# Splitting the first v tiles earlier, keeping worked-ahead tiles for behind the gates, writing the last gates in two pieces, beginning the rows by index later

## The chip, the core and the metric

The kernel runs on one core of a Trainium2 chip. The metric is the time of one execution in device microseconds. Before the change it is the median of three executions; beside these stands one profiled execution, whose trace is read below. TensorE multiplies, VectorE, ScalarE (ACT) and GpSimd (POOL) work on tiles in SBUF, SyncE (SP) issues most of the transfers, POOL those by index.

## What is computed

The reference runs two layers of a hybrid trunk: a normalised and modulated input projection, three token mixers, a gated merge, and then the part that the change touches, an expert layer with product keys. For every token, 8 heads choose 16 of 16,384 experts each, and the experts' rows of u and v are used:

```python
act = gelu(einsum('td,thkd->thk', xb, u[ib]))
out = einsum('thk,thkd->td', gb * act, v[ib])
```

with ib the chosen indices and gb a softmax over the 16 scores. The first layer has 512 tokens (256 latent, 256 of context), the second 256. The output is the latent stream after a last norm.

## The kernel before

**Dense instead of gathered.** The kernel doesn't fetch rows for most tokens. It works through all 128 tiles of 128 experts: for tile i1 it forms gelu(u x h) for all tokens, multiplies with a gate (zero for experts that a token did not choose), and adds the product with v to sums in PSUM. Products are made of three matmuls on float32r halves: a tile is split into a high part (a cast on ACT) and a low part (a subtraction on VectorE or POOL). In the first layer the first 128 tokens go another way, by index: 128 rows of u and 128 rows of v are fetched for all of them by POOL, each worked on by VectorE. The list todo holds these steps (4 groups of 32, with a step for the gelu of each group), 260 in all; function due tells how many of them are to be done by tile i1, from tile GA on over GB tiles, with a weight of 2 for tiles 0 to 15 and 26 to 111 and of 1 for the others. Dense are thus TD = 384 tokens in the first layer and 256 in the second.

**The gates.** Function spread builds the gates, 128 tokens per call, 32 (TB) per buffer stg, four per step. A step makes a one-hot tile o2 (on VectorE, one time in eight on ACT), four tiles o1 on VectorE, four matmuls into one bank of PSUM, and a copy by ACT into stg. When stg is full it is written to Gd in DRAM, 2 MB: 12 writes in the first layer, 8 in the second. Behind the last one the loop over groups of GS = 4 tiles loads Gt, the gates of four tiles, out of all blocks of Gd.

**Tiles worked ahead.** While gates are made, TensorE has work in between: early_tiles forms gelu(u x h) for the first NP = 26 tiles (NA of their results lie in pool uv, NX in pool ux), each by 8 plain float32 matmuls, which the trace records as 16, reading h2f, the unsplit copy of h. Function fill(n) advances them by n matmuls. 11 tiles (NR) go ahead of the routing, the rest is spread evenly over the steps of spread. fill and spread put their matmuls in one order by hand (at_, issue_after). Other instructions are ordered by the framework's scheduler, which keeps no strict program order among engines' queues: a load may be issued earlier than the lines say.

**Buffers.** Weight tiles are loaded into wr and split into whi and wlo, in turn from the pools in raws and parts. In the expert part the first layer has two buffers of each, the second three. dp, the pool of the last loop (gS and gacc in the first layer, then Gt with two buffers, ah, al, three each of vr, vh, vl, and four of gr for the rows by index), is opened after the pools of h2f and of the gates are closed, and so takes their room; a new tile waits for the readers of an old one that lay in its place.

**The loop.** For each tile: the activation (worked ahead, or by wload and mm3), the product with the gate on VectorE, the cast ah on ACT, the rest al on VectorE, the load and split of v in vparts, and, one tile behind, vstage: 6 matmuls per 128 tokens.

Of the kernel before, what the change touches and what calls it, by code (L numbers as in the profile page):

```python
# [22 lines left out]
TB = 32  # L23
OH = "DDDDDDDA"

GA, GB = 2, 118


PRE = ((16, 10, 11), (26, 0, 11))
HALF = ("100100", "000100")  # L30
HALF = [[int(c) for c in h] for h in HALF]
HB = 2
# [11 lines left out]
def hybrid_trunk(ctx: ExitStack, tc: tile.TileContext, xin, cin, ccol, vecs, rows, ada_w, ada_s, w_in, rpb, w_up, w_out,  # L44
                 wq, keys, u, un, v, consts, out, dbg=None):
    nc = tc.nc
    PE, ACT, DVE, POOL, SP = nc.tensor, nc.scalar, nc.vector, nc.gpsimd, nc.sync
# [11 lines left out]
    def nm(s):  # L59
        cnt[0] += 1  # L60
        return f"{s}_{cnt[0]}"
# [155 lines left out]
    def wload(src, k=8, e=None, behind=None):  # L217

        wn[0] += 1
        raw = raws[wn[0] % len(raws)].tile([128, 8, 128], F32, name=nm("wr"), tag="wr")  # L220
        last["load"] = SP.dma_start(raw[:, :k], src).ins
        p = parts[wn[0] % len(parts)]
        hi = p.tile([128, 8, 128], F32R, name=nm("whi"), tag="whi")
        lo = p.tile([128, 8, 128], F32R, name=nm("wlo"), tag="wlo")
        e = e or (DVE if wn[1] and wn[0] % wn[1] == 0 else POOL)
        with tc.issue_after(behind) if behind is not None else nullcontext():
            ACT.copy(hi[:, :k], raw[:, :k])  # L227
        if half[0]:
            DVE.tensor_tensor(lo[:, :k // 2], raw[:, :k // 2], hi[:, :k // 2], op=OP.subtract)  # L229
            e.tensor_tensor(lo[:, k // 2:k], raw[:, k // 2:k], hi[:, k // 2:k], op=OP.subtract)  # L230
        else:
            e.tensor_tensor(lo[:, :k], raw[:, :k], hi[:, :k], op=OP.subtract)  # L232
        return hi, lo
# [41 lines left out]
    for l in range(NL):  # L275
        ctx_out = l < NL - 1
        T = 512 if ctx_out else 256
        NT = T // 128
# [16 lines left out]
        with ExitStack() as st:  # L295
            npool = pool(st, "np")
            if l == 0:
# [14 lines left out]
                for s in range(2):  # L312
                    for hf in range(2):
                        p = bcast_cols(sc_[:, :, s], 4 * hf, 4, "pm")
# [83 lines left out]
        with ExitStack() as st:  # L398
# [71 lines left out]
            for j in (4, 5, 6, 7, 8, 9, 10, 11, 0, 1, 2, 3):  # L470
# [9 lines left out]
                else:  # L480
                    DVE.scalar_tensor_tensor(a, th, 1.0, a, op0=OP.add, op1=OP.mult)
                    p = PS()
# [507 lines left out]
        G0 = 128 if ctx_out else 0  # L990
        TD = T - G0
        NBK = TD // TB
        NA, NX, NR = PRE[l]
        NP = NA + NX
        uv = pool(hst, "uv", 2)
        if G0:
# [171 lines left out]
        def early_tiles():  # L1168

            for i1 in range(NP):  # L1170
                wn[0] += 1
                raw = raws[wn[0] % len(raws)].tile([128, 8, 128], F32, name=nm("wr"), tag="wr")
                SP.dma_start(raw, u[l, i1])
                p = PM()
                for k in range(8):
                    e = PE.matmul(p[:, 0:TD], raw[:, k], h2f[:, k, G0:T], start=k == 0, stop=k == 7).ins  # L1176
                    if k == 7:
                        a = act_tile(i1)
                        last["gelu"] = ACT.activation(a, p[:, 0:TD], AF.Gelu).ins  # L1179
                        pre_acts.append(a)  # L1180
                    yield e

        fills = early_tiles()
        at_ = [None, 0, 0]

        def fill(n):

            for _ in range(n):
                with tc.issue_after(at_[0]) if at_[0] is not None else nullcontext():
                    e = next(fills, None)  # L1190
                if e is None:
                    return
                at_[0] = e
                at_[1] += 1

        def spread(t, iT):

            for b in range(128 // TB):
                stg = sp2.tile([128, 128, TB], F32, name=nm("stg"), tag="stg", bufs=2)
                for c in range(TB // 4):  # L1200
                    p = PS()
                    n = TB * b + 4 * c
                    o2 = sp2.tile([128, 4, 128], F32, name=nm("o2"), tag="o2", bufs=4)
                    how = OH[c % 8]
                    if how == "A":
                        for i in range(4):
                            ACT.activation(o2[:, i], iota, AF.Abs, scale=-1.0, bias=iT[:, 2, n + i:n + i + 1])
                        ACT.activation(o2, o2, AF.Relu, scale=-1.0, bias=1.0)
                    else:
                        DVE.tensor_tensor(o2, iota.unsqueeze(1).to_broadcast([128, 4, 128]),  # L1210
                                          iT[:, 2, n:n + 4].unsqueeze(2).to_broadcast([128, 4, 128]),
                                          op=OP.is_equal)
                    for i in range(4):
                        o1 = sp2.tile([128, 128], F32, name=nm("o1"), tag="o1", bufs=8)
                        DVE.tensor_scalar(o1, iota, iT[:, 1, n + i:n + i + 1], iT[:, 0, n + i:n + i + 1],
                                          op0=OP.is_equal, op1=OP.mult)
                        with tc.issue_after(at_[0]):
                            at_[0] = PE.matmul(p[:, 128 * i:128 * i + 128], o2[:, i], o1, start=True, stop=True).ins  # L1218
                    ACT.copy(stg[:, :, 4 * c:4 * c + 4].rearrange("p i t -> p t i"),
                             p.rearrange("p (t i) -> p t i", t=4))  # L1220

                    at_[2] += 1
                    fill(8 * NR + -(-8 * (NP - NR) * at_[2] // (TD // 4)) - at_[1])
                SP.dma_start(Gd[(128 // TB) * t + b - G0 // TB], stg)

        rt_ = {}
        fill(8 * NR)
# [6 lines left out]
        with ExitStack() as st:  # L1234
            sp2 = pool(st, "sp2", side="right")
            for t in range(G0 // 128, NT):
                spread(t, rt_[t])
        it_st.close()
        hf_st.close()
# [2 lines left out]

        pst_ps = ExitStack()
        ps_pools(pst_ps, ps=8 - NPM)
        GS = 4
        half[0] = HALF[l][5]
        dp = pool(hst, "dp", 2)
        todo = []
# [52 lines left out]
                                  stop=i1 == 127 and n == 2)  # L1301

        def vparts(i1):
            vr = dp.tile([128, 1024], F32, name=nm("vr"), tag="vr", bufs=3)
            SP.dma_start(vr, v[l, i1])
            vh = dp.tile([128, 1024], F32R, name=nm("vh"), tag="vh", bufs=3)
            vl = dp.tile([128, 1024], F32R, name=nm("vl"), tag="vl", bufs=3)
            split(vr, vh, vl, e_lo=DVE)
            return vh, vl

        ntodo = len(todo)
        for g in range(128 // GS):
            Gt = dp.tile([128, NBK, GS, TB], F32, name=nm("Gt"), tag="Gt")
            SP.dma_start(Gt.rearrange("p b e t -> p b (e t)"),
                         Gd[:, :, GS * g:GS * g + GS, :].rearrange("b p e t -> p b (e t)"))
            for e in range(GS):
                i1 = GS * g + e
                if i1 < NP:
                    a = pre_acts[i1]
                else:  # L1320
                    uh, ul = wload(u[l, i1], e=DVE if ctx_out else None)
                    p = PM()
                    mm3(p[:, 0:TD], uh, ul, h2h, h2l, (G0, T))
                    a = act_tile(i1)
                    last["gelu"] = ACT.activation(a, p[:, 0:TD], AF.Gelu).ins  # L1325
                DVE.tensor_tensor(a.rearrange("p (b t) -> p b t", t=TB), a.rearrange("p (b t) -> p b t", t=TB),  # L1326
                                  Gt[:, :, e, :], op=OP.mult)
                ah = dp.tile([128, TD], F32R, name=nm("ah"), tag="ah", bufs=5)
                al = dp.tile([128, TD], F32R, name=nm("al"), tag="al", bufs=5)
                ACT.copy(ah, a)  # L1330
                ev = DVE.tensor_tensor(al, a, ah, op=OP.subtract)  # L1331
                acts.append((i1, ah, al) + vparts(i1))
                if i1:
                    vstage(*acts.pop(0))

                n = len(todo) - ntodo + due(i1)
                for f, j in todo[:n]:
                    with tc.issue_after(ev.ins):
                        f(j)
                del todo[:n]  # L1340
                if NX and i1 == NP:

                    ux_st.close()
                    xst = ExitStack()
                    xT = pool(xst, "xp", side="right").tile([128, 8, 512], F32, name=f"xr{l}")
                    SP.dma_start(xT, xs2)
            if G0 and g == 30:
                for hf in range(2):
                    p = PM()
                    for k in range(4):  # L1350
                        PE.transpose(p[:, 128 * k:128 * k + 128], gacc[:, 512 * hf + 128 * k:512 * hf + 128 * k + 128],
                                     ident)
                    for k in range(4):
                        d = 4 * hf + k
                        DVE.scalar_tensor_tensor(xT[:, d, 0:128], p[:, 128 * k:128 * k + 128], mod[:, 40 + d, 0:1],
                                                 xT[:, d, 0:128], op0=OP.mult, op1=OP.add)
# [142 lines left out]
```

## Time and profile before

| what | us |
|---|---|
| median of 3 executions | 3756.54 (3756.0 to 3765.81) |
| the profiled execution's own time | 3751.19 |
| its span, first to last instruction | 3749.4 |
| TensorE busy | 3549.1 (95% of the span) |
| VectorE busy | 2710.7 (72%) |
| ACT busy | 1553.2 (41%) |
| POOL busy | 988.5 (26%) |

All times inside the trace count from the start of the span. A busy TensorE is not a TensorE at its peak, since ends of matmuls are modelled. The gates of the first layer lie between some 1073 and 1238 us, those of the second between 2973 and 3084; the loop over the tiles follows each.

### The profile page before, as it was taken

The page shows a single profiled execution, that of the slowest core. Times are in us where ns is not written, and L with a number is a line of the kernel's source. Part 1 is how long each engine was busy: PE and PEld are TensorE (multiplying, and loading weights), DVE is VectorE, ACT ScalarE, POOL GpSimd, SP SyncE. Part 2 cuts the span into 40 slices and gives each one's busy share as a digit, 9 for nine tenths or more (in the row PEclk, how much of TensorE's full clock was granted, in tenths as well). Part 3 has the DMA queues.
Part 4 walks back from the last instruction along what each step waited for, and adds up shares of the span by engine and source line. Part 5 has one row for each costly group of instructions (what it writes and reads, how often), then busy time and mean ns, then how long its engine had stood idle before and what let it go on. Part 6 is the DMA issues. An engine that isn't in the chain of part 4 may idle for free. (4 is left out here: it accounts for less than half of the span.)

```text
span 3749.4 us, 53254 instructions
## 1 busy us (share of the span) xinstructions
PE 3549.1 (95%) x19889; PEld 3052.4 (81%) x19889; DVE 2710.7 (72%) x5479; ACT 1553.2 (41%) x2454; POOL 988.5 (26%) x761
## 2 busy tenths in 40 slices
PE   7899999898999889999999989998999999999998
PEld 4788766677778679999999977887698998999997
DVE  7767556975999777777777648687567886666666
ACT  4312554224347433333333334123655475444444
POOL 3311332333300344433443212121333100222221
PEclk9989999999999999999999999799999999999999
DMA  4211123652235899888888732224245468666664
GB/s 183 97 43 33 47 76 117 219 171 94 87 135 208 318 335 317 295 296 310 291 301 300 251 115 85 74 92 162 72 148 163 146 237 265 211 211 206 216 213 132
DMA packets 265587, 681.56 MB, mean 182 GB/s; under 512 B 20976, under 2 KB 115696, under 8 KB 261744
## 3 DMA queue, kind: packets, MB, share of 16 engines
q1 hardware_dynamic: 228464, 543.93, 43.4%
q0 software_dynamic: 36864, 134.23, 10.3%
q8 instruction: 156, 2.56, 0.3%
q14 instruction: 103, 0.84, 0.1%
HBM read 626.17 MB, written 51.90 MB: 181 GB/s over the span
## 5 line engine op out<-in xcount | busy, mean ns | idle before, releaser
L246 PE MATMUL pm<-hhi,wlo 128*128 128x256 f32 (+2 forms) x2888 | 968.8, 336 | 22.0 <-DVE wlo L229 19.8
L244 PE MATMUL pm<-hhi,whi 128*128 128x256 f32 (+2 forms) x2888 | 968.9, 336 | 16.0 <-ACT whi L227 12.8
L245 PE MATMUL pm<-hlo,whi 128*128 128x256 f32 (+2 forms) x2888 | 970.4, 336 | 1.3 <-POOL hlo L207 0.9
L227 ACT CAST whi<-wr 128x1024 fp32r<-128x1024 f32 (+1 forms) x430 | 430.3, 1001 | 865.8 <-PE pm L245 672.4
L246 PEld LDWEIGHTS pm<-hhi,wlo 128*128 128x128 f32 x2888 | 554.2, 192 | 64.9 <-DVE wlo L229 26.6
L244 PEld LDWEIGHTS pm<-hhi,whi 128*128 128x128 f32 x2888 | 554.8, 192 | 61.2 <-ACT whi L227 13.6
L245 PEld LDWEIGHTS pm<-hlo,whi 128*128 128x128 f32 x2888 | 554.7, 192 | 47.4 <-issue 5.2
L232 POOL TENSOR_TENSOR wlo<-wr,whi 128x1024 fp32r<-128x1024 f32 x124 | 300.7, 2425 | 1086.6 <-ACT whi L227 1032.5
L1300 PE MATMUL ps<-vh,ah 128*128 128x512 f32 x1280 | 401.0, 395 | 22.2 <-ACT ah L1330 13.8
L1300 PE MATMUL ps<-vl,ah 128*128 128x512 f32 x1280 | 398.9, 393 | 0.9 <-DVE vl L159 0.9
L1300 PE MATMUL ps<-vh,al 128*128 128x512 f32 x1280 | 397.9, 392 | 0.2 <-DVE al L1331 0.2
L159 DVE TENSOR_TENSOR vl<-vr,vh 128x1024 fp32r<-128x1024 f32 x256 | 313.6, 1225 | 89.9 <-ACT vh L158 89.6
L232 DVE TENSOR_TENSOR wlo<-wr,whi 128x1024 fp32r<-128x1024 f32 x181 | 223.7, 1236 | 197.1 <-ACT whi L227 196.7
L158 ACT CAST vh<-vr 128x1024 fp32r<-128x1024 f32 x256 | 268.5, 1049 | 175.2 <-PE ps L1300 107.7
L1256 POOL DMA_INDIRECT gr<-in_un_dram,gix x128 | 175.5, 1371 | 476.6 <-DVE gr L1262 231.2
L1326 DVE TENSOR_TENSOR act<-act,Gt 128x384 f32<-128x384 f32 (+1 forms) x256 | 222.2, 874 | 103.8 <-ACT act L1325 91.2
L1300 PEld LDWEIGHTS ps<-vl,ah 128*128 128x128 f32 x1280 | 241.2, 189 | 56.4 <-DVE vl L159 3.6
L1300 PEld LDWEIGHTS ps<-vh,al 128*128 128x128 f32 x1280 | 241.2, 189 | 53.1 <-DVE al L1331 0.8
L1300 PEld LDWEIGHTS ps<-vh,ah 128*128 128x128 f32 x1280 | 233.4, 190 | 61.3 <-ACT ah L1330 16.5
L1330 ACT CAST ah<-act 128x384 fp32r<-128x384 f32 (+1 forms) x256 | 117.2, 459 | 385.2 <-DVE act L1326 365.6
L1176 PE MATMUL pm<-h2f,wr 128*128 128x384 f32 (+1 forms) x832 | 251.4, 433 | 2.8 <-ACT act L1179 2.8
L1256 POOL DMA_INDIRECT gr<-in_v_dram,gix x128 | 177.6, 1387 | 279.5 <-DVE gacc L1274 239.3
(386 smaller groups left out, 5619.6 us busy)
## 6 DMA issues: line engine op xcount, KB each, us to landing
wr<-in_u_dram SPq DMA_DIRECT2D x256, 512.0 KB, 4.6
vr<-in_v_dram SPq DMA_DIRECT2D x256, 512.0 KB, 4.7
wr<-in_w_in_dram SPq DMA_DIRECT2D x130, 512.0 KB, 3.6
aw<-in_ada_w_dram SPq DMA_DIRECT2D x88, 512.0 KB, 4.3
Gd<-stg SPq DMA_DIRECT2D x20, 2048.0 KB, 7.2
Gt<-Gd SPq DMA_DIRECT2D x32, 768.0 KB, 7.6
wr<-in_wq_dram SPq DMA_DIRECT2D x32, 512.0 KB, 3.5
Gt<-Gd SPq DMA_DIRECT2D x32, 512.0 KB, 4.7
```

Of the source, the lines that this page charges most:

```text
L158: (e_hi or ACT.copy)(hi, t)
L159: (e_lo or POOL).tensor_tensor(lo, t, hi, op=OP.subtract)
L227: ACT.copy(hi[:, :k], raw[:, :k])
L232: e.tensor_tensor(lo[:, :k], raw[:, :k], hi[:, :k], op=OP.subtract)
L244: PE.matmul(p, whi[:, i, :], xhi[:, i, c0:c1], start=st, stop=False)
L245: PE.matmul(p, whi[:, i, :], xlo[:, i, c0:c1], start=False, stop=False)
L246: PE.matmul(p, wlo[:, i, :], xhi[:, i, c0:c1], start=False, stop=sp)
L1176: e = PE.matmul(p[:, 0:TD], raw[:, k], h2f[:, k, G0:T], start=k == 0, stop=k == 7).ins
L1256: POOL.indirect_dma_start(out=r, out_offset=None, in_=src, in_offset=bass.IndirectOffsetOnAxis(ap=gix[:, j:j + 1], axis=0))
L1300: PE.matmul(acc[t][hf], x1[:, c], x2[:, 512 * hf:512 * hf + 512], start=i1 == 0 and n == 0, stop=i1 == 127 and n == 2)
L1326: DVE.tensor_tensor(a.rearrange("p (b t) -> p b t", t=TB), a.rearrange("p (b t) -> p b t", t=TB), Gt[:, :, e, :], op=OP.mult)
L1330: ACT.copy(ah, a)
```

## The change

The constants get another entry, NE: 3 of the worked-ahead tiles in the first layer and 4 in the second are taken out of the even spread and are done by fill(8 * NE) behind the last matmuls of the gates. The last write of gates goes out in two transfers, the gates of the first 8 tiles and those of the other 120. Ahead of the last call of spread, the v tiles 0 and 1 are loaded and split by wload, so into wr, whi and wlo; vparts hands them out. GA and GB become 8 and 112. Number and shapes of the matmuls stay.

```diff
-GA, GB = 2, 118
+GA, GB = 8, 112
-PRE = ((16, 10, 11), (26, 0, 11))
+PRE = ((16, 10, 11, 3), (26, 0, 11, 4))
...
-                    fill(8 * NR + -(-8 * (NP - NR) * at_[2] // (TD // 4)) - at_[1])
-                SP.dma_start(Gd[(128 // TB) * t + b - G0 // TB], stg)
+                    fill(8 * NR + -(-8 * (NP - NR - NE) * at_[2] // (TD // 4)) - at_[1])
+                g = Gd[(128 // TB) * t + b - G0 // TB]
+                if at_[2] < TD // 4:
+                    SP.dma_start(g, stg)
+                else:
+                    for c in (slice(0, 2 * GS), slice(2 * GS, 128)):
+                        SP.dma_start(g[:, c], stg[:, c])
+                    fill(8 * NE)
...
             for t in range(G0 // 128, NT):
+                if t == NT - 1:
+                    vready = {}
+                    for i1 in range(2):
+                        vh, vl = wload(v[l, i1].rearrange("p (k n) -> p k n", k=8), e=DVE)
+                        vready[i1] = [x.rearrange("p k n -> p (k n)") for x in (vh, vl)]
                 spread(t, rt_[t])
...
         def vparts(i1):
+            if i1 in vready:
+                return vready.pop(i1)
```

## Rows read from the trace of the kernel before

**Rows 1.** Stretches, first layer: length, busy (instructions) of TensorE, weight loads, VectorE, ACT, POOL; clock; DMA share; GB/s

```profile
1080.00:1238.00 158.00, 158.00 (x978) 127.29 (x977) 146.10 (x449) 121.19 (x170) 0.00 (x0) 1.00 0.52 196
...
1250.00:1260.00 10.00, 5.62 (x16) 4.12 (x17) 8.88 (x15) 5.62 (x9) 1.77 (x3) 0.57 1.03 395
...
1260.00:1300.00 40.00, 35.34 (x151) 27.57 (x150) 29.98 (x48) 10.86 (x14) 18.58 (x15) 0.99 1.03 379
```

**Rows 2.** Stretches of the second layer

```profile
2975.00:3085.00 110.00, 110.00 (x763) 103.82 (x762) 103.30 (x309) 84.32 (x121) 2.77 (x1) 1.00 0.58 208
3085.00:3100.00 15.00, 7.04 (x48) 6.55 (x48) 2.97 (x6) 4.14 (x6) 4.69 (x2) 0.72 0.97 356
```

**Rows 3.** Timeline of TensorE: start, length, engine, line, count [idle before <-releaser]

```profile
1237.17 0.63 PE L244 MATMUL pm<-hhi,whi 128*128 128x384 f32 x1
...
1254.38 1.65 PE L1300 MATMUL ps<-vh,ah 128*128 128x512 f32 x3 [8.43 <-ACT vh L158]
...
3083.47 0.47 PE L244 MATMUL pm<-hhi,whi 128*128 128x256 f32 x1
...
3103.00 1.09 PE L1300 MATMUL ps<-vh,ah 128*128 128x512 f32 x4
```

**Rows 4.** Timelines, first layer: v products (first of tiles 7, 14, 15, 17), a VectorE wait

```profile
1286.07 0.73 PE L1300 MATMUL ps<-vh,ah 128*128 128x512 f32 x2 [0.61 <-ACT ah L1330]
...
1296.83 1.23 DVE L1262 SCALAR_TENSOR_TENSOR gr<-gr,htm 128x1024 f32<-128x1024 f32 x1 [2.91 <-DMA gr<-in_un_dram,gix]
...
1331.35 0.62 PE L1300 MATMUL ps<-vh,ah 128*128 128x512 f32 x2
...
1335.43 0.62 PE L1300 MATMUL ps<-vh,ah 128*128 128x512 f32 x2
...
1347.51 0.73 PE L1300 MATMUL ps<-vh,ah 128*128 128x512 f32 x2 [1.63 <-ACT ah L1330]
```

**Rows 5.** Timeline of TensorE among the gates: matmuls worked ahead, and one step's

```profile
1081.99 1.46 PE L1176 MATMUL pm<-h2f,wr 128*128 128x384 f32 x4
1083.29 1.05 PE L1218 MATMUL ps<-o,o 128*128 128x128 f32 x8
1084.18 0.81 PE L1176 MATMUL pm<-h2f,wr 128*128 128x384 f32 x2
...
2977.33 1.03 PE L1176 MATMUL pm<-h2f,wr 128*128 128x256 f32 x4
2978.19 1.05 PE L1218 MATMUL ps<-o,o 128*128 128x128 f32 x8
```

**Rows 6.** Timeline of VectorE: first o2 of the gates and the ninth step's, both layers

```profile
1073.10 0.69 DVE L1210 TENSOR_TENSOR o<-cst,iT 128x512 f32<-128x512 f32 x1 [4.85 <-ACT iT L1159]
...
1085.53 0.68 DVE L1210 TENSOR_TENSOR o<-cst,iT 128x512 f32<-128x512 f32 x1
...
2973.47 0.69 DVE L1210 TENSOR_TENSOR o<-cst,iT 128x512 f32<-128x512 f32 x1 [9.87 <-ACT iT L1159]
```

**Rows 7.** The page's costliest lines: busy, mean ns | idle before, releaser

```profile
L159 DVE TENSOR_TENSOR vl<-vr,vh 128x1024 fp32r<-128x1024 f32 x256 | 313.6, 1225 | 89.9 <-ACT vh L158 89.6
```

**Rows 8.** Loads of worked-ahead u tiles (L1173), 1070 to 1240

```profile
DMA to landing us min/median/max: 3.4/3.6/8.2
```

**Rows 9.** Timelines of SP, VectorE and ACT about the first Gt, both layers

```profile
1238.12 0.33 SPq L1224 DMA_DIRECT2D Gd<-stg  x1
...
1245.43 0.38 SPq L1314 DMA_DIRECT2D Gt<-Gd  x1
...
1251.34 1.50 DVE L1326 TENSOR_TENSOR act<-act,Gt 128x384 f32<-128x384 f32 x3 [0.87 <-DMA Gt<-Gd]
...
1251.99 1.40 ACT L1330 CAST ah<-act 128x384 fp32r<-128x384 f32 x3 [2.78 <-DVE act L1326]
...
3093.30 0.38 SPq L1314 DMA_DIRECT2D Gt<-Gd  x1
...
3098.25 1.38 DVE L1326 TENSOR_TENSOR act<-act,Gt 128x256 f32<-128x256 f32 x3 [9.31 <-DMA Gt<-Gd]
```

More of the change, by code (lines that the diff above doesn't have):

```diff
@@ L992, in hybrid_trunk @@
         NBK = TD // TB
-        NA, NX, NR = PRE[l]
+        NA, NX, NR, NE = PRE[l]
         NP = NA + NX
@@ L1181, in early_tiles @@
                     yield e
+        GS = 4
         fills = early_tiles()
@@ L1244, in hybrid_trunk @@
         ps_pools(pst_ps, ps=8 - NPM)
-        GS = 4
         half[0] = HALF[l][5]
@@ L1331, in hybrid_trunk @@
                 ev = DVE.tensor_tensor(al, a, ah, op=OP.subtract)
-                acts.append((i1, ah, al) + vparts(i1))
+                acts.append((i1, ah, al, *vparts(i1)))
                 if i1:
```

## The prediction

> **What bounds the kernel now.** I read the table of stretches first, then the timelines of the engines around the two places that the change touches, then what the tables of lines say an added instruction costs. The reader should see three things. While the gates are built, TensorE is busy without a hole, 158.0 of 158.0 us in the first layer [rows 1], 110.0 of 110.0 in the second [rows 2]. Behind the last gates there is a hole in both layers: 8.4 us before the first v product at 1254.38 in the first [rows 3], 15.00 - 7.04 = 8.0 us in the second [rows 2]. And in the first layer the v products of tiles 7 to 17 take 1347.51 - 1286.07 = 61.4 us, 6.1 each, against 1335.43 - 1331.35 = 4.08 for an undisturbed one [rows 4]: 20.6 us lost there, with the DMA share at 1.03 in the stretch where it begins [rows 1], and VectorE standing behind a row fetched by index [rows 4]. So at most some 8.4 + 8.0 + 20.6 = 37 us, 1% of the time, are within reach.
>
> **The change part by part.** I call four tokens' worth of gates (one o2, four o1, eight recorded passes on TensorE) a quad; there are 96 in the first layer, 64 in the second.
>
> *Kept tiles.* Two matmuls of a tile worked ahead take 1083.29 - 1081.99 = 1.30 us in the first layer, 0.65 each, and 2978.19 - 2977.33 = 0.86 in the second, 0.43 each; the passes of a quad take 1084.18 - 1083.29 = 0.89 [rows 5]. Taking out 3 x 8 and 4 x 8 of them relieves TensorE of 24 x 0.65 = 15.6 us and 32 x 0.43 = 13.8 us during the gates. Left are 96 x (0.89 + 0.65) = 147.8 and 64 x 0.89 + 88 x 0.43 = 94.8 us. But VectorE, running freely at the start, needs 1085.53 - 1073.10 = 12.43 us for eight quads (seven of its own, one with ACT's help) [rows 6]: 12 x 12.43 = 149.2 and 8 x 12.43 = 99.4 us. So VectorE takes over as the bound and part of the gain stays there.
>
> *v tiles split ahead.* Two subtractions of 1.22 us per layer [rows 7] go onto VectorE inside that stretch, 2.4 us; the same two, and two casts on ACT, leave the start of the v products. The loads need weight buffers that the worked-ahead tiles use. A tile lands 3.6 us after its issue in the median, 8.2 at worst [rows 8]; in the first layer each kept-up tile has eight quads, 12.4 us, to cover a load, cast and subtraction, in the second there are three buffers and the tile behind the two v tiles has to wait for the one in use. I take 1 us of delay per layer, between 0 and 8.2 (one worst landing). The end of the gates is then 1073.10 + 149.2 + 2.4 + 1.1 (last passes and fill) + 1 = 1226.8 against 1237.2, where the u products of tile 26 start now [rows 3]; second layer 2973.47 [rows 6] + 99.4 + 2.4 + 1.1 + 1 = 3077.4 against 3083.5 [rows 3].
>
> *Behind the gates.* The kept tiles take 15.6 and 13.8 us. The second of them can only be loaded when the last one before it is done, together with the last gates' write: up to 8.2 us [rows 8] against 8 x 0.65 = 5.2 of cover, so 3.0 us of waiting in the first layer (0 to 3.0), and 0.7 in the second, where two are loaded ahead. They end at 1245.4 and 3091.9. What is late next is **Gt**. h2f, which the kept tiles read, takes 8 x 512 x 4 bytes = 16 KB of a partition in the first layer, and dp is opened where h2f stood: gS and gacc (4.5 KB), then two Gt of 6 KB. In the second it is 8 KB, and dp begins with two Gt of 4 KB. So the first two Gt lie on h2f, and their loads have to wait for the last matmul that reads it. Now nobody notices, because Gt waits for the gates' write anyway, 1245.43 - 1238.12 = 7.3 us [rows 9], and h2f is long free. After the change the kept tiles are the later ones, by some 10 us, and behind the waiting Gt on SP's queue stand the loads of v tiles 2 to 4. From Gt's issue to VectorE's first product take 1251.34 - 1245.43 = 5.9 us and 3098.25 - 3093.30 = 5.0 [rows 9]; the cast of ah starts 0.65 later and takes under 0.5, 1.1 together. First v product: 1245.4 + 7.0 = 1252.4, against 1254.4 now; second layer 3091.9 + 6.1 = 3098.0 against 3103.0 [rows 3].
>
> *What has not been done by then.* Now TensorE fills the hole with u products of tiles 26 and 27, 1254.38 - 8.43 - 1237.17 = 8.8 us [rows 3], and with three of them in the second layer (2/3 of the columns, 2.9 us each). wload puts the two split v tiles into whi and wlo, and of those the first layer has two: tiles 26 and 27 can't be split before the first v tiles are used. The second layer has three, so one u tile remains. Outstanding are 8.8 and 5.8 us: 1252.4 + 8.8 - 1254.4 = **6.8 us lost** in the first layer, 3098.0 + 5.8 - 3103.0 = **0.8 us lost** in the second, with 0.9 for a restart at half clock **1.7**. (The first layer's restart costs 5.62 - 16 x 4.08 / 18 = 2.0 us now [rows 1] and after as well; for the second's shorter hole I take 0.9 between 0 and 2.0.)
>
> *Two pieces.* The first write has 128 x 1 KB, and Gt of the first two groups needs only that of the last gates. Its issue costs SP another 0.33 us [rows 9], off the path. With Gt held by h2f it gains nothing: cost and gain 0; without the hold it is in rival A.
>
> *Rows begun later.* 260 steps spread over tiles 2 to 119 (weight 2 up to tile 15, then 1 to tile 25, then 2) are 2.39 per heavy tile; from tile 8 they are 260 x 2 / 206 = 2.52. Before, heavy tiles begin at 2 and TensorE first stands at tile 7 [rows 4]: five are absorbed by what is prepared ahead, and ten then lose 20.6 us, 2.1 each. After, there are eight heavy tiles, 8 to 15. If five are absorbed again, three lose 6.2 us: **14.4 us gained**. The bounds: none lost (20.6 gained), all eight lost (16.5, 4.1 gained). From tile 26 on TensorE is full either way, so the rate of 2.52 for 2.39 has cover; without it, 86 tiles x 0.13 x 1.22 us = 13.6.
>
> *Sum.* +6.8 + 1.7 - 14.4 = -5.9 us. The profiled execution took 3751.19 (span 3749.4), which would become 3745.3; it lies 5.35 under the median of 3756.54. I set the sum against the median: **3751 us**, rounded.
>
> **A rule on the clock.** After the hole the granted clock of the stretch in the second layer is 0.72, a mix of the 1.2 and 2.4 GHz levels [rows 2], and 0.57 where the v products begin in the first [rows 1], so both holes are paid twice, and I left 0.9 us for a shorter one. The Trainium skill ("TensorE: Matmul & The Clock Gate", What's actually happening) holds that the throttled level is the default and activity lifts it. By that rule a hole that is filled gives its restart back and the 0.9 us would be 0; the trace shows the lower clock behind a hole and agrees so far, and the sum would be 3750.
>
> **The rivals.**
> *A, Gt isn't held.* If Gt can be loaded while the kept tiles run, the first v product follows them at once: 7.0 us less in the first layer, about 3 in the second (where one u product covers part of the 6.1), and 2.0 + 0.9 of restarts. 3750.6 - 13 = **3737**. For it: Gt is due about 1 + 7.3 + 7.0 = 15 us behind the last gates, within the kept tiles' 18.6. Against it: the sizes above. The Trainium skill ("Perfetto Trace Analysis", DMA Optimizations) says that a split transfer may let work start sooner where DMA engines are generally idle; here the share is 1.03 from 1250 on [rows 1], which speaks against that condition.
> *B, the loss moves instead of shrinking.* All eight heavy tiles lose 2.1 us; 16.5 instead of 6.2: **3761**. For it: the rate per heavy tile rises. Against it: six light tiles ahead, in which loads can run ahead.
> *C, slower.* VectorE and ACT work in order. If the subtraction of a split v tile stands ahead of o1 work before its tile has landed, everything for the gates stops: 8.2 us per tile, less 3.1 for two quads of o1 in store (eight buffers), so 5.1 x 2 tiles x 2 layers = 20 us: **3771**. It decides from where the landing is later than the place in VectorE's order, by more than 3.1 us. For it: the v load's buffer frees late. Against it: 3.6 us in the median [rows 8].
>
> **How the numbers follow.** Forecast 0.48, A 0.20, B 0.20, C 0.12. This kernel's time can be told from no change from about 0.3%, 11.3 us, on. A is faster by more; of the forecast's spread (0 to 3 us for loads, 4.1 to 20.6 for the rows) some 0.15 is too. Faster 0.35. C, and 0.02 of B with a delayed load, are slower: 0.14. Same 0.51. The range goes from A with all heavy tiles absorbed, 3737 - 6 = 3731, to near C, 3769, which leaves 2 in 10 out.
>
> **What would show it.** Right: VectorE without waits during the gates, whose last write is issued some 10 us earlier in the first layer and 6 in the second; the kept tiles straight behind; Gt issued within 1 us of their last matmul; then a hole of some 7 us; u of tile 26 behind the first v products in the first layer; the first hole among the v products at tile 12 or later. Wrong: Gt issued while kept tiles run (A); 6 us per tile from tile 8 on (B); VectorE waiting on a whi cast among the last gates (C). The forecast fails if the order on SP's queue differs from what I took.

## The result, and the profile after

The changed kernel takes 3780.1 us (median of 7 executions, 3772.15 to 3787.11) where the kernel before, in 7 executions, has its median of 3756.54 again. The ratio is 1.0063, with a 95% interval of 1.0045 to 1.0081: slower by 0.6%, some 24 us. I had predicted 3751, range 3731 to 3769. The profiled execution of after took 3785.43 us; its span of 3783.7 is 34.3 longer than that of before. The profile of before lies some 5 us under its median, that of after some 5 us above, so the rows overstate the loss by about 10 us.

First the stretches about the two places, as in [rows 1, 2]. Columns: length, busy time (and instructions) of TensorE, weight loads, VectorE, ACT, POOL, then granted clock, DMA share, GB/s.

```profile
1085.50:1243.50 158.00, 147.22 (x928) 119.53 (x928) 145.21 (x450) 119.85 (x167) 0.00 (x0) 0.97 0.52 190
...
1252.00:1266.00 14.00, 13.36 (x32) 7.36 (x32) 0.00 (x0) 0.98 (x2) 3.33 (x4) 0.80 0.58 200
1266.00:1276.00 10.00, 3.74 (x9) 2.96 (x10) 4.95 (x9) 3.70 (x6) 0.00 (x0) 0.59 0.96 297
...
2999.20:3109.20 110.00, 105.00 (x714) 96.35 (x715) 100.94 (x312) 83.03 (x118) 0.00 (x0) 0.98 0.57 209
3122.00:3132.00 10.00, 5.16 (x13) 4.11 (x14) 7.08 (x12) 4.68 (x8) 2.34 (x1) 0.66 0.89 283
```

TensorE, which had no hole among the gates of the first layer [rows 1], now stands 158 - 147.22 = 10.8 us there; and the hole behind the gates is still there in both layers, at a clock of 0.59 and 0.66. What TensorE waited for in the first layer between 1078 and 1400 us (in all, times, longest), after, and of the same table of before the line that matters here:

```profile
PE pm L1176 <- DMA wr<-in_u_dram: 15.2, 2, 10.8
PE ps L1312 <- ACT ah L1344: 6.9, 1, 6.9
PE ps L1312 <- DVE vl L159: 4.2, 4, 1.5
```
```profile
PE ps L1300 <- ACT ah L1330: 12.7, 5, 5.3
```

The first line is new: twice a tile worked ahead had not landed. The second is the hole before the first v product. The third is all that is left of the holes among the v products, where before ACT's cast ah was waited for 12.7 us in five places. Timeline of SP, ACT, VectorE and TensorE about the longest wait (start, length, engine, line, [idle before <- releaser]):

```profile
1156.03 0.38 SPq L1173 DMA_DIRECT2D wr<-in_u_dram  x1
...
1168.23 0.81 PE L1176 MATMUL pm<-h2f,wr 128*128 128x384 f32 x2
1168.33 13.43 SPq L221 DMA_DIRECT2D wr<-in_v_dram  x2
...
1177.45 1.06 ACT L227 CAST whi<-wr 128x1024 fp32r<-128x1024 f32 x1
...
1179.18 0.81 PE L1176 MATMUL pm<-h2f,wr 128*128 128x384 f32 x2
...
1180.08 1.32 DVE L232 TENSOR_TENSOR wlo<-wr,whi 128x1024 fp32r<-128x1024 f32 x1
...
1181.81 0.42 SPq L1227 DMA_DIRECT2D Gd<-stg  x1
1182.34 5.87 SPq L1173 DMA_DIRECT2D wr<-in_u_dram  x2
...
1191.65 1.65 PE L1176 MATMUL pm<-h2f,wr 128*128 128x384 f32 x2 [10.77 <-DMA wr<-in_u_dram]
1193.09 1.92 PE L1219 MATMUL ps<-o,o 128*128 128x128 f32 x8
...
1193.76 1.63 DVE L1216 TENSOR_SCALAR o<-cst,iT 128x128 f32<-128x128 f32 x4 [5.91 <-PE ps L1219]
```

The first v load is issued at 1168.33; the second, the other of x2, ends that group at 1168.33 + 13.43 = 1181.76. It takes the weight buffer of the first and waits until that is split: the cast stands on ACT at 1177.45, the subtraction on VectorE, behind work for the gates, ends at 1180.08 + 1.32 = 1181.40. SP takes one thing after the other: a write of gates and the next u tile's load stand behind the waiting v load, though neither has to do with it. The u tile is issued at 1182.34 and TensorE gets it at 1191.65, having stood for 10.77 us, and its next eight matmuls of the gates take 1.92 us where such eight take 1.05 [rows 5].

The queue is the smaller part of that stall. The load of 1182.34 waits on the semaphores of the load of 1156.03 and of TensorE, so its buffer is that of the u tile before it, which TensorE works on from 1168.23 to 1179.18 + 0.81 = 1179.99. Before that it could not have been issued by any queue; SP's order added 1182.34 - 1179.99 = 2.3 us. The rest is a load without a lead. The tile before was loaded 12.2 us ahead of its first matmul (1156.03 and 1168.23), while the other buffer was in use; now the v tiles have that other buffer, one behind the other, until the second is split at 1187.86, so the u tile's own way from issue to landing, 9.3 us, lies open. (In the changed kernel loads of worked-ahead tiles land after 8.1 us in the median, most of them issued straight behind a write of gates; before it was 3.6 [rows 8].)

The rest of the first layer, and the same places of the second:

```profile
1241.65 5.97 PE L1176 MATMUL pm<-h2f,wr 128*128 128x384 f32 x18
1252.01 13.36 PE L1176 MATMUL pm<-h2f,wr 128*128 128x384 f32 x32 [4.39 <-DMA wr<-in_u_dram]
...
1265.40 0.38 SPq L1328 DMA_DIRECT2D Gt<-Gd  x1
...
1272.26 1.22 PE L1312 MATMUL ps<-whi,ah 128*128 128x512 f32 x2 [6.89 <-ACT ah L1344]
...
3051.83 1.26 PE L1219 MATMUL ps<-o,o 128*128 128x128 f32 x8 [1.74 <-DVE o L1216]
...
3060.19 0.70 PE L1176 MATMUL pm<-h2f,wr 128*128 128x256 f32 x2 [1.93 <-DMA wr<-in_u_dram]
...
3103.29 14.67 PE L1176 MATMUL pm<-h2f,wr 128*128 128x256 f32 x66
...
3119.39 0.39 SPq L1328 DMA_DIRECT2D Gt<-Gd  x1
...
3126.84 1.22 PE L1312 MATMUL ps<-whi,ah 128*128 128x512 f32 x2 [4.95 <-ACT ah L1344]
```

The kept tiles run until 1252.01 + 13.36 = 1265.37, Gt is issued at 1265.40, and the first v product follows 6.9 us later, a wait as long as the prediction had it, only 20 us later on the clock.

Where the 34.3 us of the two profiles lie: 5.5 ahead of the first gates, in code that is the same; 5.5 from the first layer's gates to its last v product; **13.7 between that and the second layer's gates, where no line was changed**; 9.2 from there to the last v product; 0.4 behind it.

### The profile page after: what moved, and what is told of

Its sections match the earlier page's. It is cut to its first block, busy times and chain, and to the rows that moved or that the text cites. A ratio compares the mean times of both kernels' runs of the same rounds, so it can differ in the third digit from the quotient of the medians.

```text
span 3783.7 us, 53293 instructions
## 1 busy us (share of the span) xinstructions
PE 3573.8 (94%) x19889; PEld 3066.2 (81%) x19889; DVE 2707.3 (72%) x5479; ACT 1552.5 (41%) x2454; POOL 991.8 (26%) x761
## 5 line engine op out<-in xcount | busy, mean ns | idle before, releaser
L1312 PE MATMUL ps<-vl,ah 128*128 128x512 f32 x1260 | 391.0, 391 | 5.0 <-DVE vl L159 4.9
L1312 PE MATMUL ps<-vh,ah 128*128 128x512 f32 x1260 | 391.6, 392 | 0.2 <-ACT vh L158 0.2
L1312 PE MATMUL ps<-vh,al 128*128 128x512 f32 x1260 | 389.9, 390 | 0.0
L1176 PE MATMUL pm<-h2f,wr 128*128 128x384 f32 (+1 forms) x832 | 260.4, 444 | 19.9 <-DMA wr<-in_u_dram 17.1
L230 POOL TENSOR_TENSOR wlo<-wr,whi 128x512 fp32r<-128x512 f32 (+1 forms) x97 | 158.3, 1633 | 344.1 <-ACT whi L227 339.9
```

The lines of the kernel that those rows point to most:

```text
L1312: PE.matmul(acc[t][hf], x1[:, c], x2[:, 512 * hf:512 * hf + 512], start=i1 == 0 and n == 0, stop=i1 == 127 and n == 2)
```

## The experiments

Three theories. *One*: the v tiles ahead block SP's queue and hold buffers. *Two*: the kept tiles cost it, since Gt waits for the last of them. *Three*: the 13.7 us come from a side effect. wload counts its calls in wn[0] and takes the buffer by that count; the two calls made ahead shift the count by two, which matters where three buffers are in rotation, as in two later stages of the second layer. (By the count's parity it also chooses between VectorE and POOL for a subtraction; a shift of two leaves that alone.) Each kernel below was timed against the kernel before on the same chip; a ratio of 0.001 is 3.8 us. The changed kernel's is 1.0063. A difference between two ratios carries both intervals, some 0.003 or 10 us either way.

**The rows alone.** The kernel before with the constants of the rows:

```diff
-GA, GB = 2, 118
+GA, GB = 8, 112
```

> The kernel before with the rows by index begun at tile 8 instead of 2 and nothing else. If the step on the rows in the prediction is right (20.6 us lost at v products 7 to 17 before, some 6 after), it is 10 to 20 us faster than before, ratio 0.995 to 0.997, and the whole loss of the change lies in its other parts, some 36 us of them. If the gain seen in the trace of after (from 17.9 + 8.8 us behind at the first v product to 11.0 at the end of the v products) belongs to the other parts, it is within 3 us of before.

Measured: 1.0003 [0.9983, 1.0022]: nothing, where I had 14.4 us of gain. What TensorE waited for from the gates to 1400 us, with the rows begun later:

```profile
PE ps L1300 <- ACT vh L158: 12.7, 2, 8.9
PE ps L1300 <- DVE vl L159: 9.5, 7, 3.2
```

The waits for ah, 12.7 us before, are gone; the 8.9 is the old hole behind the gates; in their place come 12.7 - 8.9 = 3.8 us for vh and 9.5 for vl, the two halves of a v tile. The loss moved, as in rival B.

**No v tiles ahead.** The changed kernel without them:

```diff
-                    for i1 in range(2):
-                        vh, vl = wload(v[l, i1].rearrange("p (k n) -> p k n", k=8), e=DVE)
-                        vready[i1] = [x.rearrange("p k n -> p (k n)") for x in (vh, vl)]
```

> The changed kernel without the two v tiles split ahead; kept tiles, the write in two pieces and the later rows stay. Theory 1 (the v loads ahead block SP's queue, stop TensorE for 10.8 us in the first layer, and keep the u tiles 26 and 27 out of their buffers): the stall in the last gates goes, u products fill the hole behind the kept tiles, and the time is 25 to 45 us under the changed kernel (3735 to 3755). Theory 2 (the kept tiles cost it, since Gt waits for the last of them): under 12 us faster than the changed kernel. Theory 3 (13.7 us between the two layers come from the count of weight loads, shifted by two from the v loads on): here the count is not shifted, and the start of the second layer's gates comes back to within 5 us of where the first layer's end puts it.

Measured: 0.9986 [0.9967, 1.0006], 3748.8 us; against the changed kernel's ratio that is 0.0077, some 29 us less. TensorE's waits in the same stretch:

```profile
PE pm L1176 <- DMA wr<-in_u_dram: 4.2, 1, 4.2
PE ps L1309 <- ACT vh L158: 3.5, 1, 3.5
PE ps L1309 <- DVE vl L159: 2.5, 4, 1.0
```

The 10.8 is gone, the u products fill the hole, and 2.5 us is left among the v products. Without the two calls of wload the count isn't shifted either, so the 29 us belong to theories one and three together; two explains at most what is left.

**No kept tiles.** The changed kernel with

```diff
-PRE = ((16, 10, 11, 3), (26, 0, 11, 4))
+PRE = ((16, 10, 11, 0), (26, 0, 11, 0))
```

> The changed kernel with no tile worked ahead kept for behind the gates (0 and 0 instead of 3 and 4); v tiles split ahead, the write in two pieces and the later rows stay. Theory 2 (the kept tiles cost it): 10 to 25 us under the changed kernel. Theory 1 (the v loads ahead cost it): the tile behind the v loads still stands behind them on SP, and nothing covers the hole behind the gates any more, since u tiles 26 and 27 have no buffers: some 5 to 15 us above the changed kernel.

Measured: 1.0051 [1.0030, 1.0072], some 4 us less than the changed kernel, inside the intervals. It was neither as two nor as one had it. The trace shows both effects at once: the stall stays, and the hole gets longer.

```profile
1177.62 10.24 SPq L221 DMA_DIRECT2D wr<-in_v_dram  x2
...
1188.19 0.81 PE L1176 MATMUL pm<-h2f,wr 128*128 128x384 f32 x2
...
1189.91 21.06 SPq L1173 DMA_DIRECT2D wr<-in_u_dram  x3
...
1198.88 2.93 PE L1176 MATMUL pm<-h2f,wr 128*128 128x384 f32 x4 [8.99 <-DMA wr<-in_u_dram]
...
1268.42 1.22 PE L1312 MATMUL ps<-whi,ah 128*128 128x512 f32 x2 [13.94 <-ACT ah L1344]
```

With whi and wlo held by v tiles no u product fills the 13.9 us; the kept tiles had covered that hole, so they are not the loss.

This trace also parts the queue from the buffer. The second v load is out at 1177.62 + 10.24 = 1187.86, before the u tile in work ends at 1188.19 + 0.81 = 1189.00. The next u tile's load, which needs that tile's buffer, follows at 1189.91, 0.9 us behind it, and TensorE still stands for 9.0 us. So the stall comes almost whole where the v load holds up next to nothing on SP.

**Gt on room of its own.** The changed kernel with

```diff
+        gtp = pool(hst, "gtp", 2)
...
-            Gt = dp.tile([128, NBK, GS, TB], F32, name=nm("Gt"), tag="Gt")
+            Gt = gtp.tile([128, NBK, GS, TB], F32, name=nm("Gt"), tag="Gt")
```

> The changed kernel with the buffers of Gt in a pool of their own that doesn't lie on h2f. Theory 2 in its narrow form (Gt waits for the last kept matmul because it lies on the room of h2f): Gt is issued while the kept tiles run, the hole before the first v product shrinks from 6.9 to under 2 us in the first layer and from 5.0 to about 1 in the second, 9 to 12 us under the changed kernel with the restarts. Rival: something else holds Gt or the first product (the gates' write, ah and al, which now lie on h2f): the holes stay above 4 us and the time within 4 us of the changed kernel.

Measured: 1.0053 [1.0030, 1.0076]; the medians are 7 us apart, the ratios 4. Gt goes out at 1250.24, ahead of the second kept tile, and the first product follows the last kept matmul within 1 us:

```profile
1250.24 10.37 SPq L1329 DMA_DIRECT2D Gt<-Gd  x3
...
1254.31 11.96 PE L1177 MATMUL pm<-h2f,wr 128*128 128x384 f32 x32 [4.54 <-DMA wr<-in_u_dram]
...
1267.25 0.73 PE L1313 MATMUL ps<-whi,ah 128*128 128x512 f32 x2 [0.98 <-ACT ah L1345]
...
1269.77 1.96 DVE L1341 TENSOR_TENSOR act<-act,Gt 128x384 f32<-128x384 f32 x4 [1.43 <-DMA Gt<-Gd]
...
1271.64 1.49 DVE L1346 TENSOR_TENSOR al<-act,ah 128x384 fp32r<-128x384 f32 x3
...
1272.25 1.22 PE L1313 MATMUL ps<-whi,al 128*128 128x512 f32 x2 [3.81 <-DVE al L1346]
```

So Gt was held by h2f, and rival A's condition can be made. It brings some 4 us, within the intervals, where A had 13: of the 6.9 us, 3.81 come back four matmuls later, since al stands in VectorE's order behind products with the gates, one of which waits 1.43 us for the next Gt.

**The count alone.** The kernel before with two lines behind the first layer's gates:

```diff
+        if l == 0:
+            wn[0] += 2
```

> The kernel before with the count of weight loads, wn[0], raised by two behind the first layer's gates and nothing else: the work is the same, but with three weight buffers in rotation, as two later stages of the second layer have, it begins with another buffer. Theory 3 (the 13.7 us that the changed kernel loses between the first layer's last v product and the second layer's gates come from this shift): 7 to 13 us slower than before, lost between the layers, in the same two places as in the changed kernel. Rival (they are scatter from one execution to the next): within 3 us of before, and no delay in those two places.

Measured: 1.0034 [1.0018, 1.0051], some 13 us (7 to 19), with not one instruction more. TensorE's projections in the second layer, from the first product of line 917 to the first transpose of line 1031, before and with the count shifted (count | busy, mean ns | idle):

```profile
L246 PE MATMUL pm<-hhi,wlo 128*128 128x256 f32 x200 | 57.2, 286 | 0.0
```
```profile
L246 PE MATMUL pm<-hhi,wlo 128*128 128x256 f32 x208 | 59.5, 286 | 0.0
```

That stretch lasts 198.4 us before and 206.8 with the shift. It lasts 196.6 to 200.7 in the nine kernels of this study whose count isn't shifted, and 206.4 to 208.3 in the five where it is, the changed kernel (207.8) among them. Eight more of each product, one weight tile, lie in it with the shift, work that otherwise is done earlier. Of the 8.4 us, 5.1 are busy time of TensorE (195.9 for 190.8) and 3.3 are waits. Work that only moved is no loss if the stretch ahead, from the first layer's last v product on, gets shorter by as much; it lasts 434.1 to 456.0 us in the kernels without the shift, so that the traces can't tell. That the shift costs 13 us rests on the timed executions.

**The count put back.** The changed kernel with

```diff
                         vready[i1] = [x.rearrange("p k n -> p (k n)") for x in (vh, vl)]
+                    if l == 0:
+                        wn[0] -= 2
```

> The changed kernel with the count of weight loads put back by two behind the two v tiles of the first layer, so that the second layer's stages use their buffers in the order of the kernel before. Theory 3: 7 to 13 us under the changed kernel, 3767 to 3773. Rival (scatter): within 3 us of the changed kernel.

Measured: 1.0039 [1.0019, 1.0059], 0.0024 or 9 us under the changed kernel; the stretch lasts 198.2 us again. The gain is of the size that was expected, but by itself not clear of the two intervals. The stretch follows the count in both directions; in time, theory three is shown by the count alone, and this run agrees with it.

**The old rows on the changed kernel**, GA, GB = 2, 118:

> The changed kernel with the rows by index begun at tile 2 as before. Rows alone, on the kernel before, gained 3.7 us of the 14.4 that I predicted, though the v products of the changed kernel catch up by 15.7. If the later rows gain only when v tiles are prepared ahead of the products (the two changes need each other): 9 to 16 us slower than the changed kernel. If the catching up comes from the v tiles ahead and the kept tiles and not from the rows: within 4 us of the changed kernel.

Measured: 1.0101 [1.0076, 1.0127], 0.0038 or 14 us above the changed kernel, little more than the two intervals leave open.

**The old rows and no v tiles ahead**, so that the kept tiles (and the two pieces) stand alone:

> No v tiles split ahead, rows by index begun at tile 2 as before, kept tiles and the write in two pieces: the kept tiles alone on the kernel before. If the later rows gain only where something else gives the first v tiles a lead (rows alone gained 3.7 us in the traces, on the changed kernel they gain 13): 5 to 13 us slower than the kernel without v tiles ahead, near the kernel before or slower. If the kept tiles alone carry the 13.5 us of the first layer: within 3 us of the kernel without v tiles ahead.

Measured: 1.0022 [1.0005, 1.0039], against 0.9986 with the later rows. With these runs a square is full: neither, 1; rows alone 1.0003; kept tiles alone 1.0022; both 0.9986. What is clear of the intervals is that the kept tiles do better with the later rows than with the old ones, by 14 us; that both together beat the kernel before, or the rows alone, is not. With kept tiles and old rows, ah is waited for again, as before:

```profile
PE ps L1309 <- ACT ah L1341: 13.7, 6, 5.0
```

What the kept tiles add I read from when POOL begins to fetch rows: 1238.37, which is 21.7 us ahead of the first v product, without v tiles ahead; 1254.23, 8.5 us ahead, with the rows alone. In the latter the fetches meet the first Gt and v loads, with a DMA share of 1.03 from 1250 to 1270, against 0.86 in the other. With kept tiles and the old rows POOL begins 22.4 us ahead as well, so that this lead alone isn't enough. That it is the cause where the rows are late is argued; no run holds the fetches back by themselves.

**v tiles with buffers of their own.** The changed kernel, v tiles split ahead as there, but loaded elsewhere, and wn[0] untouched:

```diff
+            vwp = pool(st, "vwp", 2, side="right")
...
-                        vh, vl = wload(v[l, i1].rearrange("p (k n) -> p k n", k=8), e=DVE)
-                        vready[i1] = [x.rearrange("p k n -> p (k n)") for x in (vh, vl)]
+                        vr = vwp.tile([128, 1024], F32, name=nm("vwr"), tag="vwr")
+                        SP.dma_start(vr, v[l, i1])
+                        p = parts[(wn[0] + 1 + i1) % len(parts)]
+                        vh, vl = (p.tile([128, 8, 128], F32R, name=nm(n), tag=n).rearrange("p k n -> p (k n)")
+                                  for n in ("whi", "wlo"))
+                        ACT.copy(vh, vr)
+                        DVE.tensor_tensor(vl, vr, vh, op=OP.subtract)
+                        vready[i1] = vh, vl
```

> The changed kernel, v tiles split ahead as there, but loaded into two buffers of their own instead of the weight buffers that the tiles worked ahead use; the count of weight loads is not touched. Theory 1 (the second v tile's load waits on SP's queue for a weight buffer, and the gates' write and the next u tile's load behind it come late, so that TensorE stands 10.8 us): in the first layer SP issues both v loads at once, the stall goes, and the last gates are written about 10 us earlier against the gates' start. With the count left alone (9 to 13 us by the two runs on it) that is 20 to 28 us under the changed kernel, 3752 to 3760. Rival (the stall comes from ACT's cast or VectorE's subtraction standing in their queues, as in rival C of the prediction): the stall stays, over 6 us, and only the count's 9 to 13 us are gained.

Measured: 0.9997 [0.9982, 1.0013], 3758.2 us, some 25 under the changed kernel. With free buffers both loads are issued together, and the scheduler puts them ahead of the first write of gates:

```profile
1078.34 0.90 SPq L1250 DMA_DIRECT2D vwr<-in_v_dram  x2
...
1231.16 5.97 PE L1176 MATMUL pm<-h2f,wr 128*128 128x384 f32 x18
...
1241.53 13.35 PE L1176 MATMUL pm<-h2f,wr 128*128 128x384 f32 x32 [4.40 <-DMA wr<-in_u_dram]
...
1261.55 1.22 PE L1319 MATMUL ps<-whi,ah 128*128 128x512 f32 x2 [6.67 <-ACT ah L1351]
```

The gates end at 1231.2 instead of 1241.7, and no wait among them is over 1 us. ACT and VectorE make the same casts and subtractions as in the changed kernel, the first subtraction at 1177.2 us where there it stood at 1180.08, and they hold up nothing. The u tiles have both weight buffers again: the load of 1168.6 is for the tile whose matmuls begin at 1182.6. Theory one holds, and the rival to it falls. This kernel takes away the wait on SP and the use of the weight buffers together; which of them weighs more is seen above, 2.3 of 10.8 us for the queue in the changed kernel, 0.9 of 9.0 without kept tiles.

**The first layer only**: no v tiles ahead, PRE = ((16, 10, 11, 3), (26, 0, 11, 0)), later rows.

> No v tiles split ahead, later rows, the kept tiles and the two pieces in the first layer alone; the second layer keeps no tile. In the trace without v tiles ahead the touched part of the first layer was 13.5 us shorter than in the kernel before, that of the second 4.8 longer. If the two add up: 9 to 14 us under before, ratio 0.996 to 0.998, and about 5 us under the kernel without v tiles ahead. If the second layer's 4.8 are scatter or come from the rows: no better than the kernel without v tiles ahead.

Measured: 0.9983 [0.9964, 1.0002], 3749.0 us: a little less gain than the 0.996 to 0.998 expected, with an interval that reaches into it, and it can't be told from 0.9986 without v tiles ahead.

**The same with Gt on room of its own:**

> Kept tiles, two pieces and later rows in the first layer, the second as before, no v tiles ahead, and Gt in buffers of its own. If Gt on the room of h2f is what ends the hole there too: Gt is issued some 12 us earlier, the hole of 3.1 us before the first v product of the first layer shrinks under 1, the first products come 5 to 8 us earlier and u tiles fill in later: 3 to 5 us under the kernel with the first layer only, 9 to 12 under the kernel before. If the first v tile's load decides (it is behind Gt on SP, and its buffer lies on the same room): no gain, within 2 us.

Measured: 0.9985 [0.9969, 1.0000]. No gain: the last hole is then 5.3 us before u tile 26, plus 1.5 before the first v product, where it was 0.6 and 3.1.

**One write instead of two**, without v tiles ahead:

> The kernel without v tiles ahead, with the last gates written in one piece instead of two. The prediction put the two pieces at 0, since Gt is issued only when the kept tiles are done, long behind either landing: within 4 us of the kernel without v tiles ahead, and Gt's issue at the same distance from the last kept matmul. Rival (the pieces bring the last gates early enough that rows or Gt start sooner): 5 us or more slower without them, with Gt issued later than the last kept matmul.

Measured: 0.9978 [0.9958, 0.9999] against 0.9986: the same. Gt is issued at 1250.48 there, 0.1 us behind the last kept matmul, as with two pieces. Hardly one of the kernels is better than the one before: the best four have 0.9978 to 0.9986, 5 to 8 us, with intervals that end at 0.9999 to 1.0006. All four have later rows, kept tiles and no v tiles ahead, and in their profiles the first layer, from its gates to its last v product, is 10.4 to 13.5 us shorter than in the kernel before.

## Why the prediction was wrong

Its steps beside the profiles, each as the difference to before in us, the layer's parts counted from the layer's first matmul of the gates:

| step | predicted | changed kernel | v tiles in own buffers |
|---|---|---|---|
| end of the gates, first layer | -10.4 | -0.6 | -11.4 |
| first v product | -2.0 | +12.4 | +1.4 |
| last v product | -7.6 | +5.5 | -5.5 |
| from there to the second layer's gates | 0 | +13.7 | -5.1 |
| end of the gates, second layer | -6.1 | -4.6 | -6.7 |
| first v product | -5.0 | -0.8 | -6.7 |
| last v product | +1.7 | +9.2 | +5.9 |

**The step that failed first** is "I take 1 us of delay per layer, between 0 and 8.2 (one worst landing)" for the v loads, with its premise that in the first layer "each kept-up tile has eight quads, 12.4 us, to cover a load, cast and subtraction". The bound took a load's price to be its own landing. But the v tiles took the place of u tiles: both went through one of the two weight buffers, from 1168.33 to 1187.86, and the next u tile, with only the other buffer, had no cover at all. TensorE stood for 10.8 us: 2.3 for the order on SP and 9.3 for a load that could not start earlier, less 0.9 of gate matmuls that were still to do. I had asked for the order on SP's queue at the very end ("fails if the order on SP's queue differs from what I took") and had not asked whose turn in the buffers the v loads would take. Rival C saw that the v load's buffer may free late, but had the wrong victim: it priced a standstill of VectorE, 5.1 us per tile, while what stood was TensorE for want of a u tile. With buffers of their own for the v tiles the end of the gates came at -11.4, so the working from VectorE's 12.43 us per eight quads [rows 6] was right.

**The second** was no step at all: the count wn[0], put at nothing, 13 us (7 to 19) by the run on it alone. Calling wload twice more was costed by what it issues, not by the state that it leaves. The kernel before has the line that says so, a buffer taken by the count modulo the number of buffers. How the other phase makes one weight tile late is not settled; the traces show that it does, and where.

The two missed terms, 10.8 at the end of the gates (-0.6 against -11.4 in the table) and 13, make some +18 of the predicted -5.9; measured were +24 [+17, +30]. With both taken away the kernel is at -1 [-7, +5], an interval with the predicted -5.9 in it; in its profile the two layers' parts come to -5.5 + 5.9 = +0.4, where the prediction had -7.6 + 1.7.

**The rows** were right in size by luck. In the profile of after the v products catch up 12.4 + 8.8 - 5.5 = 15.7 us, in the runs on the changed kernel 14, predicted were 14.4. But I derived it from the number of heavy tiles alone, and alone it is worth nothing (1.0003). There the loss moved, as rival B had it at 0.20. The working had a slip too: heavy tiles from 7 to 15 are nine, not ten, which makes 13.7 of the 14.4.

**Behind the gates.** Gt held by h2f was right, to the place: in the first layer it was issued 0.03 us behind the last kept matmul. The kept tiles waited 4.4 us for their load (predicted 3.0, bounded by 3.0) and ran 13.4 us after it instead of 10.4, since TensorE restarted at a lower clock, 0.80 on average there, which I had not charged. In the second layer one u product stood in the hole, as told, where before there were three. The first v product came 4.2 us later than predicted: 1.2 up to the first kept matmul, from stalls at the gates, and 0.9 from the kept tiles, whose 0.7 of waiting did not come; 1.4 since Gt was issued at 3119.39, 1.4 us behind the last kept matmul and behind u loads on SP; 1.4 from Gt to the product. The restart cost 2.3 where I took 0.9.

On the clock, the Trainium skill ("TensorE: Matmul & The Clock Gate", What's actually happening) calls the throttled level the default, lifted by activity; the traces agree: behind each hole of 4.4 to 10.8 us the same matmuls take nearly twice as long at first (1.92 for 1.05). I let it argue for 0 in place of 0.9; the hole wasn't filled, and it cost 2.3. The Trainium skill ("Perfetto Trace Analysis", DMA Optimizations) also says that it may make sense to give loads and stores different issuing engines. No run here tries that; it would bear on the 2.3 us for which a load, a store and a load shared SP.

## What to carry to other kernels

Before moving a load forward, ask which buffer it takes, whose turn that was and who frees it, then list what its queue would issue while it waits. The price is what the others lose by it, not its own landing time: here the next load lost its lead of 12 us, and 2.3 us on the queue. Buffers of its own took both away (10.8 us). A helper that counts its calls is state: an extra call shifts every later choice made by the count, even a thousand microseconds on, so compare stretches with unchanged code too. What a change is worth can hang on another one, so isolated runs don't add up (the later rows took the ratio from 1 to 1.0003 alone, but from 1.0022 to 0.9986 with the kept tiles).

## What I had not expected of the hardware

A shift of a buffer's phase, without an instruction more, costs 0.34% (0.18% to 0.51%). And unchanged code scatters: from the last v product of the first layer to the second layer's gates the profiles of the nine kernels with an unshifted count take 736.3 to 759.9 us, a spread as large as the whole loss; a single pair of profiles would not have told the 13.7 us from it. Only the short stretch that lasted 196.6 to 200.7 in all of them did, and the timed executions.
